# Matmuls in the source's order, finish and sample tokens as streams of their own, paired BK*AR

## The chip, the cores and the metric

The kernel runs on one core of one Trainium2 chip. The metric is device time in microseconds (us) of one execution. A core has TensorE (PE in the profile, its weight loads PEld), VectorE (DVE), ScalarE (ACT), GpSimd (POOL) and SyncE (SP, which here issues most DMAs). Each engine has an instruction stream of its own; semaphores order them. Matmuls write to PSUM, which has eight banks of 128 partitions x 512 float32.

## What is computed

One layer of a hybrid encoder on 1024 prompt tokens and 32 sample tokens. Cut to what matters:

```python
xn = rms_norm(x, norm_g)
proj = xn @ w_in                                   # 2048 -> 8320 columns
q, k, v, g_att, p_rw, g_rw = split(proj)
q, k = rope(rms_norm(q)), rope(rms_norm(k))        # 8 heads, two maps of 64 each
s = q @ k.T * 64 ** -0.5, masked by chunks of 64
p = softmax(s); attn = p[map 0] - lam * p[map 1]   # differential attention
o = rms_norm(attn @ v, subln_g) * (1 - lam_init)
att_out = o * silu(g_att)
# RWKV-7: per token, 16 heads of 64
S = S * w_t + (S @ a_t) b_t + v_t k_t;  y = S @ r_t
y = layer_norm(y) + bonus;  rw_out = y * silu(g_rw)
return x + [att_out, rw_out] @ w_out, and k, v, the last S, the last projected row
```

The sample tokens attend to 256 cached keys besides their own and begin from a given state.

## The kernel before

All data is float32 and lies with features on the partitions and tokens on the free axis. The tokens are done in two halves: the first (A) has prompt tokens 0 to 511 and the 32 sample tokens, 544 columns in two blocks of 288 and 256; the second (B) has prompt tokens 512 to 1023, 512 columns. `proj` multiplies a block of 128 output features by 16 blocks of the contraction. To keep the precision, weights and activations are split into a high and a low part in a faster matmul format (`wh`, `wl` in `split_w`, `xh`, `xl` in `split_x`), and each product is three matmuls: 96 matmuls a projection in A, 48 in B. Matmuls of plain float32 (those of the recurrence among them) appear as two records each, and transposes by PE as one.

The main loop goes over u = 0 to 15, eight heads of A and then eight of B. A head has eight projections in this order: q, k, v, attention's gate, the three inputs of the recurrence, its gate. After the heads come 16 output projections of A and 16 of B.

All other work of PE is woven into the projections. It is written as Python generators, queued in six streams: `chs` (`rw_chain`, the recurrence by chunks of 64 tokens), `dns` (`rw_down`, what a chain needs), `qks` (q, k and v), `pos` (`rw_post`), `ats` (`att_task`), `los` (`rw_decay`). A generator yields a delay, or a delay with a PSUM bank (`"am"` or `"Y"`), or a condition. The builder keeps a clock of PE's time, `clk`, to which each matmul adds its cost; a stream is taken up again when the clock has passed its delay and, if it named a bank, the time at which that bank is taken to be free. The delays stand in the table `LAT` in ns (line 39), by name and half: c1, c2, c3 are the three steps of a chain's cycle, for example. `pump` tries all streams; `proj` calls it every second or fourth block of the contraction and tries the chain's stream after each (lines 372 to 376). `drain` runs a stream until a named task is done, and moves the clock if it must; the loop drains attention of head u-1 after q's projection of head u (line 1006).

What the source does in this order is not the order in which PE works. The framework's scheduler orders the instructions of every engine when the program is built, by dependences and by its own estimate of times. So `LAT` gives the earliest place of a step and the scheduler may set it later.

The steps that the change touches:

- One cycle of `rw_chain` (lines 878 to 920): a matmul of `AR` with the state (`ch<-Sw,AR`); ACT copies `RS` from the bank (893), DVE adds `xs` in two instructions (896), ACT makes `SP` (899); a matmul `ch<-xs,TT` (901); ACT and DVE copy `UV` (902, 903); two matmuls `ch<-UV,MM` (906); DVE makes the new state `Sw` (908) and Y (916). Ahead of the cycles come transposes of v and three steps on 32 x 32 and 64 x 64 blocks (850 to 865), which wait for the solved blocks by DMA and a transpose on DVE (846).
- In `rw_down` `BK` times `AR` is done for four chunks at a time (754 to 768): first the four products of the partitions 0 to 63 into the bank Y, then, after Y is free, those of 64 to 127. DVE masks each result into MM (765). DVE then solves triangular systems in 31 steps of two instructions (784, 786).
- `att_task` goes over four query tiles of 128 in turn (527): scores into the two banks `sc`, softmax, the difference of the two maps (563), transposes into `sc` (570), a copy (571, 573), products with v into `am` (581), then `att_finish`. That squares the bank's values with a sum (504), takes the reciprocal root, multiplies by the row's factor (507), copies the bank with this scale (509), waits (511), transposes (513) and multiplies into `sg` (514). The next tile begins after it. In A the sample tokens follow as a fifth tile (583 to 618), in the buffer of E0.
- A PSUM tile is allocated anew for each use (`PT("am", 1)`, `PT("Y", 1)`, `PT("ch", 1)`, `PT("sc", 1)`), with one buffer a name.

```python
            elif isinstance(y, tuple):
                self.at, self.am = clk[0] + y[0], y[1]
```

Of the kernel before, what the change touches and what calls it, by code (L numbers as in the profile page):

```python
# [31 lines left out]
SCALE = 64 ** -0.5  # L32
# [6 lines left out]
LAT = dict(qkA=6246, qkB=2980, vA=9930, vB=9930, finA=1949, finB=3111, sc1A=1400, sc1B=1260, scAA=3566, scAB=3056, sc2A=3181, sc2B=3736, aTA=640, aTB=873, smp0A=2190, smp0B=3000, smp1A=4433, smp1B=7243, smp2A=1452, smp2B=1100, decA=3192, decB=6684, rnA=2646, rnB=1890, msA=8290, msB=8364, ms2A=2463, ms2B=1016, bk0A=1758, bk0B=1724, att0A=4044, att0B=1900, am2A=304, am2B=265, Y2A=1822, Y2B=1994, boA=1350, boB=3075, bktA=2250, bktB=2000, ttA=13941, ttB=14740, t10A=2258, t10B=1343, c0A=1052, c0B=2447, c1A=2162, c1B=1936, c2A=1122, c2B=978, c3A=1014, c3B=1276, postA=6000, postB=4636, dmA=5550, dmB=4110, solveA=31509, solveB=33325, am=900, Y=2208, scA=5863, sc1=2240, sc2=2872)  # L39
# [7 lines left out]
def build(tc, I, O):  # L47
# [18 lines left out]

    def am():
        ready["am"] = None
        return PT("am", 1)

    def ym():
        ready["Y"] = None
        return PT("Y", 1)
# [9 lines left out]
    def mm(out, lhsT, rhs, start=True, stop=True):  # L83
# [7 lines left out]
        clk[0] += max(0.4375 * n + 6.0, load) if rhs.dtype == F32R else 2 * max(0.84 * n, load)  # L91
# [12 lines left out]
    class Stream:  # L104
# [21 lines left out]
        def step(self):  # L126
# [20 lines left out]
            elif isinstance(y, tuple):  # L147
                self.at, self.am = clk[0] + y[0], y[1]
# [4 lines left out]
    chs, dns, los, qks, ats, pos = (Stream() for _ in range(6))  # L153
    streams = (chs, dns, qks, pos, ats, los)
# [346 lines left out]
    def att_finish(half, o_ps, m, il, sg, c0):  # L501
        oj = T([128, 128], "os", bufs=2)
        sm = T([128, 2], "sm", bufs=4)
        S.activation(oj[:m], o_ps, AF.Square, scale=il, accum_out=sm[:m, 0:1])
        rsqrt(sm[:m, 1:2], sm[:m, 0:1], 1.0 / 128, b_eps[:m])
        if not isinstance(il, float):
            V.tensor_tensor(sm[:m, 1:2], sm[:m, 1:2], il, op=ALU.mult)
        os_ = T([128, 128], "os", bufs=2)
        S.activation(os_[:m], o_ps, AF.Copy, scale=sm[:m, 1:2])
        ready["am"] = clk[0] + lat("fin", half)  # L510
        yield lat("fin", half), "am"
        pt = am()
        tr(pt[:, 0:m], os_[:m], ident[:m, :m])
        V.scalar_tensor_tensor(sg[:, c0:c0 + m], pt[:, 0:m], subg, sg[:, c0:c0 + m],
                               ALU.mult, ALU.mult)

    def att_task(half, h, st):
# [7 lines left out]

        yield lat("att0", half)
        for j in range(4):
# [7 lines left out]
            E = [T([128, 1024], "E0"), T([128, 1024], "E1")]  # L535
            mx = T([128, 2], "sm", bufs=4)
            l = T([128, 4], "l", bufs=2)
            if half == 0:
                sc = PT("sc", 1, (128, 2, 512))
# [9 lines left out]
            else:  # L549
                for c in range(2):  # L550
                    if c:
                        yield lat("sc1", half) + 2 * nk
                    sc = PT("sc", 1, (128, 2, 512)).rearrange("p a b -> p (a b)")
# [13 lines left out]
            aT = T([128, 8, 128], "E1")  # L567
            pt = PT("sc", 1, (128, 8, 128))
# [13 lines left out]
            yield from att_finish(half, po[:, :128], 128, l[:, 2:3], sg, qc)  # L582
        if half == 0:
            qb, ksm = st["qb"], st["ksm"]
            sm_ = T([128, 1024], "E0")
            ck = sm_[:, 0:256]
            dma(ck, I["ckT"][h])
# [572 lines left out]
```

## Time and profile before

| | |
|---|---|
| median of 3 runs | 2612.56 us (2609.12 to 2618.03) |
| the profiled execution, its own time | 2613.46 us |
| its span, first to last instruction | 2611.7 us |
| TensorE busy | 2549.7 us, 98% |
| weight loads busy | 2220.1 us, 85% |
| VectorE busy | 1892.0 us, 72% |
| ScalarE busy | 1349.6 us, 52% |
| GpSimd busy | 415.1 us, 16% |
| granted clock of TensorE, mean | 0.995 of full |

Matmuls are pipelined. The time of one in the profile includes its way through the array, with a modelled end, so the times of neighbours overlap, and a busy PE can still be late. The distance from one start to the next tells more than the duration. Idle time is given with what ended it, as far as the semaphores tell.

### The profile page before, as it was taken

The numbers are of one execution on the slowest core, as the hardware profiler recorded it, in microseconds if no ns is written. First come the engines' busy times: TensorE is split into PE (matmuls) and PEld (weight loads), VectorE is DVE, ScalarE is ACT, GpSimd is POOL, SyncE is SP. The second block draws the span as 40 slices with busy tenths as digits, with TensorE's granted clock in tenths as the row PEclk, the third lists the DMA queues.
The fourth block names the chain that finished last, engine by engine and source line by source line (L and its number), as shares of the span: only waits on it lengthen the run. The fifth ranks groups of instructions, "written<-read, shape, count | busy, mean of one in ns | idle before, by whom it ended". The sixth has DMA issues, their size and how long they took to land. (4 is left out here: it accounts for less than half of the span.)

```text
span 2611.7 us, 49090 instructions
## 1 busy us (share of the span) xinstructions
PE 2549.7 (98%) x17128; PEld 2220.1 (85%) x17128; DVE 1892.0 (72%) x5768; ACT 1349.6 (52%) x3138; POOL 415.1 (16%) x949
## 2 busy tenths in 40 slices
PE   7999999999999999999999999999999999999999
PEld 7999999999898999877777777777777778999887
DVE  7576877777777787788787887788878888753432
ACT  6455555555555655565555555555555556332321
POOL 3211111111111111111111111111111111111000
PEclk9999999999999999999999999999999999999999
DMA  4433332324242524353332323232324244544443
GB/s 156 119 102 94 93 103 84 110 82 115 75 122 80 170 72 122 98 153 100 98 98 87 103 83 106 85 111 81 114 81 115 77 132 118 176 148 140 137 142 108
DMA packets 198665, 286.74 MB, mean 110 GB/s; under 512 B 102097, under 2 KB 115921, under 8 KB 198417
## 3 DMA queue, kind: packets, MB, share of 16 engines
q0 software_dynamic: 51088, 169.12, 21.8%
q1 hardware_dynamic: 147328, 114.47, 15.5%
q8 instruction: 136, 2.23, 0.4%
q14 instruction: 113, 0.92, 0.1%
HBM read 228.11 MB, written 37.51 MB: 102 GB/s over the span
## 5 line engine op out<-in xcount | busy, mean ns | idle before, releaser
L92 PE MATMUL pj<-xh,wh 128*128 128x256 f32 (+2 forms) x3888 | 1294.2, 333 | 7.7 <-ACT xh L248 6.7
L92 PE MATMUL pj<-xl,wh 128*128 128x256 f32 (+2 forms) x3888 | 1274.7, 328 | 5.0 <-DVE xl L249 5.0
L92 PE MATMUL pj<-xh,wl 128*128 128x256 f32 (+2 forms) x3888 | 1272.5, 327 | 1.1 <-DVE wl L225 1.1
L92 PEld LDWEIGHTS pj<-xh,wh 128*128 128x128 f32 x3888 | 735.7, 189 | 61.2 <-ACT xh L248 7.0
L92 PEld LDWEIGHTS pj<-xl,wh 128*128 128x128 f32 x3888 | 736.2, 189 | 52.5 <-DVE xl L249 8.8
L92 PEld LDWEIGHTS pj<-xh,wl 128*128 128x128 f32 x3888 | 735.4, 189 | 52.4 <-DVE wl L225 2.1
L224 ACT CAST wh<-wr 128x512 fp32r<-128x512 f32 x584 | 360.6, 618 | 471.8 <-PE pj L92 420.1
L225 DVE TENSOR_TENSOR wl<-wr,wh 128x512 fp32r<-128x512 f32 x584 | 401.2, 688 | 193.5 <-ACT wh L224 162.9
L231 POOL DMA_DIRECT2D wr<-w_in x517 | 278.3, 538 | 1639.8 <-DVE wl L225 492.2
L786 DVE TENSOR_TENSOR ts<-tm,ts 64x54 f32<-64x54 f32 (+35 forms) x992 | 198.2, 200 | 15.1
L784 DVE TENSOR_TENSOR tm<-ts,ms 64x54 f32<-64x54 f32 (+35 forms) x992 | 197.7, 199 | 14.5 <-DMA ts<-tinit 0.2
L92 PEld LDWEIGHTS ch<-UV,MM 64*64 64x64 f32 (+2 forms) x1632 | 111.5, 145 | 38.1 <-DVE UV L903 9.2
L92 PE MATMUL ch<-UV,MM 64*64 64x64 f32 (+2 forms) x1632 | 128.9, 231 | 8.0 <-DVE UV L846 5.1
L899 ACT ACTIVATE SP<-Sw,PL 64x64 f32<-64x64 f32 x256 | 88.3, 345 | 91.2 <-DVE Sw L908 78.1
L225 DVE TENSOR_TENSOR wl<-MM,wh 128x512 fp32r<-128x512 f32 x64 | 44.0, 689 | 89.1 <-ACT wh L224 89.1
L224 ACT CAST wh<-MM 128x512 fp32r<-128x512 f32 x64 | 39.6, 620 | 128.9 <-PE pj L92 123.3
L896 DVE TENSOR_TENSOR xs<-ch,MM 64x64 f32<-64x64 f32 x272 | 58.6, 216 | 50.2 <-ACT RS L893 45.7
L908 DVE SCALAR_TENSOR_TENSOR Sw<-ch,PL,SP 64x64 f32<-64x64 f32 x256 | 70.7, 276 | 23.2 <-PE ch L92 16.7
L92 PE MATMUL am<-Vt,E 128*128 128x128 f32 (+1 forms) x592 | 84.7, 280 | 1.8 <-ACT wh L224 1.1
L92 PE MATMUL Y<-AR,BK 64*128 64x128 f32 x544 | 84.8, 290 | 0.7 <-DVE MM L765 0.6
L92 PEld LDWEIGHTS Y<-AR,BK 64*128 64x128 f32 x544 | 67.5, 188 | 19.8 <-issue 9.1
L92 PEld LDWEIGHTS am<-Vt,E 128*128 128x128 f32 (+1 forms) x592 | 73.5, 189 | 8.7 <-issue 2.6
(303 smaller groups left out, 3127.9 us busy)
## 6 DMA issues: line engine op xcount, KB each, us to landing
wr<-w_in POOLq DMA_DIRECT2D x517, 256.0 KB, 3.2
wr<-w_out POOLq DMA_DIRECT2D x64, 256.0 KB, 3.6
MM<-w_out POOLq DMA_DIRECT2D x32, 512.0 KB, 4.0
t<-xB SPq DMA_DIRECT2D x32, 256.0 KB
ms<-dm SPq DMA_DIRECT2D x96, 64.0 KB
t<-t SPq DMA_DIRECT2D x64, 68.0 KB
t<-mixd SPq DMA_DIRECT2D x16, 272.0 KB
t<-xA SPq DMA_DIRECT2D x16, 272.0 KB
```

What stands on the lines that cost most here:

```text
L92: PE.matmul(out, lhsT, rhs, start=start, stop=stop)
L224: S.copy(wh, raw)
L225: V.tensor_tensor(wl, raw, wh.bitcast(F32), op=ALU.subtract)
L231: q.dma_start(raw, wsrc[:, g * 512:(g + 1) * 512].rearrange("p (k f) -> p k f", k=4))
L784: V.tensor_tensor(tm, ts_[:, 0:qn, s:s + 1].to_broadcast([R * nb, qn, m]), ms[:, s:s + 1, s + 1:32].to_broadcast([R * nb, qn, m]), op=ALU. ...
L786: V.tensor_tensor(ts_[:, 0:qn, s + 1:32], tm, ts_[:, 0:qn, s + 1:32], op=ALU.add)
L896: V.tensor_tensor(xs[64 * h:64 * h + 64], ch[low, 64 * h:64 * h + 64], MM[low, c, h, 0:64], op=ALU.add)
L899: S.activation(SP[:, h, :], S_[hr, h, :], AF.Copy, scale=PL[hr, 0, gc:gc + 1])
L908: V.scalar_tensor_tensor(S_[hr, h, :], ch[low, 192 + 64 * h:256 + 64 * h], PL[low, h, gc:gc + 1], SP[:, h, :], ALU.mult, ALU.add)
```

## The change

PE's instructions are issued in the order of the source; the other engines are still ordered by the scheduler. The delays in `LAT` are set anew, most of them longer, a few shorter (t10A, t10B, c0B, Y2B), with new names for two steps (x0, bk). A wait may name two banks. Banks are allocated once and held. BK*AR alternates between the partitions 0 to 63, into Y, and 64 to 127, into `am`, and waits for both banks. The last part of `att_finish` becomes a task of a new stream, `fis`, and its first part reads the bank once and works on the copy. The sample tokens become a task of a new stream, `sms`, in parts of E0 and E1 that the first half's tiles do not use; `att_task` waits at its end for both. In the chain's cycle `xs` comes ahead of `RS`.

```diff
-LAT = dict(..., finA=1949, finB=3111, sc1A=1400, sc1B=1260, scAA=3566, ..., sc2B=3736, aTA=640, aTB=873, smp0A=2190, ..., smp1A=4433, ..., rnB=1890, ms2A=2463, ms2B=1016, bk0A=1758, bk0B=1724, ..., am2A=304, ..., ttA=13941, ttB=14740, t10A=2258, t10B=1343, c0A=1052, c0B=2447, c1A=2162, c1B=1936, c2A=1122, c2B=978, c3A=1014, c3B=1276, ..., am=900, Y=2208, ...)
+LAT = dict(..., finA=5000, finB=5000, sc1A=1400, sc1B=3600, scAA=8400, ..., sc2B=4400, aTA=2500, aTB=3000, smp0A=3600, ..., smp1A=9500, ..., rnB=6200, ms2A=2600, ms2B=3000, bk0A=7300, bk0B=6000, ..., am2A=2100, ..., ttA=27000, ttB=25500, t10A=1000, t10B=1000, c0A=1300, c0B=1700, c1A=2500, c1B=2300, c2A=2500, c2B=2500, c3A=1700, c3B=1800, ..., am=1500, Y=2208, ..., x0A=1000, x0B=1000, bkA=2600, bkB=3000)
...
+    held = {}
+    def bank(tag, shape=(128, 512)):
+        if tag not in held:
+            held[tag] = PT(tag, 1, shape)
+        return held[tag]
...
-            return max(self.at, ready[self.am]) if self.am else self.at
+            return max(self.at, *(ready[a] for a in self.am)) if self.am else self.at
...
-    chs, dns, los, qks, ats, pos = (Stream() for _ in range(6))
-    streams = (chs, dns, qks, pos, ats, los)
+    chs, dns, los, qks, ats, pos, fis, sms = (Stream() for _ in range(8))
+    streams = (chs, dns, qks, pos, fis, ats, sms, los)
...
-    def att_finish(half, o_ps, m, il, sg, c0):
+    def att_finish(half, h, name, o_ps, m, il, st, c0):
         oj = T([128, 128], "os", bufs=2)
+        S.activation(oj[:m], o_ps, AF.Copy, scale=il)
         sm = T([128, 2], "sm", bufs=4)
-        S.activation(oj[:m], o_ps, AF.Square, scale=il, accum_out=sm[:m, 0:1])
+        os_ = T([128, 128], "os", bufs=2)
+        S.activation(os_[:m], oj[:m], AF.Square, accum_out=sm[:m, 0:1])
         rsqrt(sm[:m, 1:2], sm[:m, 0:1], 1.0 / 128, b_eps[:m])
-        if not isinstance(il, float):
-            V.tensor_tensor(sm[:m, 1:2], sm[:m, 1:2], il, op=ALU.mult)
-        os_ = T([128, 128], "os", bufs=2)
-        S.activation(os_[:m], o_ps, AF.Copy, scale=sm[:m, 1:2])
-        ready["am"] = clk[0] + lat("fin", half)
-        yield lat("fin", half), "am"
-        pt = am()
-        tr(pt[:, 0:m], os_[:m], ident[:m, :m])
-        V.scalar_tensor_tensor(sg[:, c0:c0 + m], pt[:, 0:m], subg, sg[:, c0:c0 + m],
-                               ALU.mult, ALU.mult)
+        S.activation(os_[:m], oj[:m], AF.Copy, scale=sm[:m, 1:2])
+        def fin(born):
+            yield lambda: "sg" in st
+            yield max(0, born + lat("fin", half) - clk[0]), "am"
+            pt = am()
+            tr(pt[:, 0:m], os_[:m], ident[:m, :m])
+            sg = st["sg"]
+            V.scalar_tensor_tensor(sg[:, c0:c0 + m], pt[:, 0:m], subg, sg[:, c0:c0 + m],
+                                   ALU.mult, ALU.mult)
+        fis.add(("fin", half, h, name), fin(clk[0]))
...
+    def sample_task(h, st):
+        Et, qb, ksm, Vt = (st[a] for a in ("Et", "qb", "ksm", "Vt"))
+        ck = Et[0][:, 512:768]
...
+        att_finish(0, h, 4, po[0:32, :128], 32, 1.0, st, 256)
...
+        if half == 0:
+            sms.add(("smp", h), sample_task(h, st))
...
             yield lat("aT", half), "am"
-            if j == 0:
-                yield lambda: "sg" in st
-                sg = st["sg"]
-                yield lat("am2", half), "am"
...
-            yield from att_finish(half, po[:, :128], 128, l[:, 2:3], sg, qc)
+            att_finish(half, h, j, po[:, :128], 128, l[:, 2:3], st, qc)
...
-        dma(mixd[half][h], sg)
+            yield lambda: ("smp", h) in sms.done
+        yield lambda: all(("fin", half, h, j) in fis.done for j in range(5 - half))
+        dma(mixd[half][h], st["sg"])
...
+            yield lat(key, half), "Y", "am"
+            key = "ms2"
+            ps2 = (ym(), am())
+            for j in range(m):
+                for h, hr in enumerate((low, high)):
+                    mm(ps2[h][:, 128 * j:128 * j + 128],
+                       BK[hr, c0 + j].rearrange("p a t -> p (a t)"),
+                       AR[hr, c0 + j].rearrange("p a t -> p (a t)"), ways=2)
             for h in range(2):
-                yield lat(key, half), "Y"
-                key = "ms2"
-                hr = (low, high)[h]
-                p = ym()
-                for j in range(m):
-                    mm(p[:, 128 * j:128 * j + 128],
...
             mm(ch[:, 0:128], AR[:, c].rearrange("p a t -> p (a t)"), Sf)
-            RS = T([128, 128], "RS")
-            S.copy(RS[high], ch[high, 0:128])
             xs = T([128, 64], "xs")
             for h in range(2):
                 V.tensor_tensor(xs[64 * h:64 * h + 64], ch[low, 64 * h:64 * h + 64], MM[low, c, h, 0:64], op=ALU.add)
+            RS = T([128, 128], "RS")
+            S.copy(RS[high], ch[high, 0:128])
...
     with tile.TileContext(nc) as tc:
-        build(tc, I, O)
+        with tc.manual_schedule(engines={mybir.EngineType.PE}):
+            build(tc, I, O)
```

## Rows read from the trace of the kernel before

**Rows 1.** The page: the span, and busy time of each engine.

```profile
span 2611.7 us, 49090 instructions
...
PE 2549.7 (98%) x17128; PEld 2220.1 (85%) x17128; DVE 1892.0 (72%) x5768; ACT 1349.6 (52%) x3138; POOL 415.1 (16%) x949
```

**Rows 2.** Table of stretches: stretch, length, busy us of each engine, clock, DMA.

```profile
260.00:700.00 440.00, 430.00 (x3465) 402.91 (x3464) 333.36 (x1096) 237.42 (x596) 73.15 (x187) 1.00 0.33 95
1300.00:1800.00 500.00, 489.52 (x2715) 385.26 (x2713) 400.94 (x1261) 274.73 (x633) 74.82 (x164) 0.99 0.33 95
2450.00:2600.00 150.00, 150.00 (x651) 121.97 (x651) 45.73 (x68) 34.00 (x55) 13.72 (x26) 1.00 0.43 135
```

**Rows 3.** The chain that ended last, its last two links: start, length, what.

```profile
2342.09 265.94 PE pj L92 x1476
2608.05 0.69 DVE t L968
```

**Rows 4.** Timeline of PE around one BK*AR: start us, length us, what.

```profile
1571.45 0.39 PE L92 MATMUL pj<-xl,wh 128*128 128x512 f32 x1
1571.67 0.40 PE L92 MATMUL pj<-xh,wl 128*128 128x512 f32 x1
1572.00 1.16 PE L92 MATMUL Y<-AR,BK 64*128 64x128 f32 x8
1573.09 0.50 PE L92 MATMUL pj<-xh,wh 128*128 128x512 f32 x1
1573.43 0.40 PE L92 MATMUL pj<-xl,wh 128*128 128x512 f32 x1
```

**Rows 5.** List of waits: who waited for whom, us in total, times, longest.

```profile
DVE xs L896 <- ACT RS L893: 45.7, 40, 4.2
...
PE ch L92 <- DVE xs L896: 7.0, 16, 1.6
PE pj L92 <- ACT xh L248: 6.7, 1, 6.7
...
PE ch L92 <- DVE UV L846: 5.1, 7, 1.2
```

**Rows 6.** Groups by line and shape, PE: BK*AR.

```profile
L92 PE MATMUL Y<-AR,BK 64*128 64x128 f32 x544 | 84.8, 290 | 0.7 <-DVE MM L765 0.6
```

**Rows 7.** Timeline of PE, second half, without the projections: chain and attention.

```profile
1746.67 0.68 PE L92 MATMUL ch<-UV,MM 64*64 64x64 f32 x16
...
1748.24 0.46 PE L92 MATMUL ch<-Sw,AR 128*128 128x128 f32 x2
1750.40 0.41 PE L92 MATMUL ch<-xs,TT 128*128 128x64 f32 x2
...
1753.72 0.57 PE L92 MATMUL ch<-UV,MM 128*128 128x64 f32 x4
...
1756.13 1.06 PE L92 MATMUL am<-Vt,E 128*128 128x128 f32 x8
...
1760.56 0.48 PE L92 MATMUL sc<-Ks,Qd 128*128 128x512 f32 x1
...
1761.22 0.27 PE L97 MATMUL am<-cst,os 128*128 128x128 f32 x1
```

**Rows 8.** Timeline of DVE after the BK*AR of rows 4.

```profile
1578.25 0.68 DVE L765 TENSOR_TENSOR MM<-Y,cst 128x512 f32<-128x512 f32 x1
```

**Rows 9.** Timeline of ACT and of DVE in the cycle of rows 7.

```profile
1748.74 0.26 ACT L893 COPY RS<-ch 64x128 f32<-64x128 f32 x1 [0.60 <-PE ch L92]
...
1750.08 0.22 DVE L896 TENSOR_TENSOR xs<-ch,MM 64x64 f32<-64x64 f32 x1
...
1753.29 0.23 DVE L903 COPY UV<-ch 64x64 f32<-64x64 f32 x1
...
1754.84 0.28 DVE L908 SCALAR_TENSOR_TENSOR Sw<-ch,PL,SP 64x64 f32<-64x64 f32 x1
```

**Rows 10.** Timeline of PE at the end of head 11's attention.

```profile
1697.28 0.33 PE L97 MATMUL am<-cst,os 128*128 128x128 f32 x1
...
1699.07 0.39 PE L92 MATMUL pj<-xh,wh 128*128 128x512 f32 x1
```

More of the change, by code (lines that the diff above doesn't have):

```diff
@@ L65, in build, with scores2 @@
     ready = {"am": 0.0, "Y": 0.0}
+    held = {}
[3 more added lines that the diff above has]
+        return held[tag]
     def am():
         ready["am"] = None
-        return PT("am", 1)
+        return bank("am")
     def ym():
         ready["Y"] = None
-        return PT("Y", 1)
+        return bank("Y")
+    def scores2():
+        return bank("sc", (128, 2, 512))
     mode = [(128, 128)]
@@ L81, in shaped, with mm @@
             mode[0] = now
-    def mm(out, lhsT, rhs, start=True, stop=True):
+    def mm(out, lhsT, rhs, start=True, stop=True, ways=1):
         n, m = 1, 1
@@ new lines, in sample_task @@
+    def sample_task(h, st):
+        Et, qb, ksm, Vt = (st[a] for a in ("Et", "qb", "ksm", "Vt"))
+        ck = Et[0][:, 512:768]
+        dma(ck, I["ckT"][h])
+        cv = Et[0][:, 768:1024].rearrange("p (j d) -> p j d", j=2)
+        dma(cv, I["cv"][:, h, :].rearrange("(j p) d -> p j d", p=128))
+        yield lat("smp0", 0), "am"
+        p = am()
+        mm(p[0:64, 0:256], qb, ck)
+        mm(p[0:64, 256:288], qb, ksm)
+        sx = T([64, 4], "sx")
+        V.tensor_reduce(sx[:, 0:1], p[0:64, 0:288], AX.X, ALU.max)
+        V.tensor_scalar(sx[:, 0:1], sx[:, 0:1], -SCALE, None, ALU.mult)
+        es = Et[1][0:64, 512:800]
+        S.activation(es, p[0:64, 0:288], AF.Exp, bias=sx[:, 0:1], scale=SCALE,
+                     accum_out=sx[:, 1:2])
+        V.reciprocal(sx[:, 2:3], sx[:, 1:2])
+        cmb = T([64, 32], "cmb")
+        V.tensor_scalar(cmb, idst, sx[:, 2:3], lamcol, ALU.mult, ALU.mult)
+        yield lat("smp1", 0), "am"
+        p = am()
+        for j in range(3):
+            m = 128 if j < 2 else 32
+            mm(p[:m, 32 * j:32 * j + 32], es[:, 128 * j:128 * j + m], cmb)
+        at = Et[1][:, 800:896].rearrange("p (j q) -> p j q", j=3)
+        V.tensor_copy(at[:, 0:2, :], p[:, 0:64].rearrange("p (a b) -> p a b", a=2))
+        V.tensor_copy(at[0:32, 2, :], p[0:32, 64:96])
+        yield lat("smp2", 0), "am"
+        po = am()
+        for j in range(3):
+            if j < 2:
+                mm(po[0:32, :128], at[:, j, :], cv[:, j, :], start=(j == 0), stop=False)
+            else:
+                mm(po[0:32, :128], at[0:32, 2, :], Vt[0:32, 4, :], start=False)
+        att_finish(0, h, 4, po[0:32, :128], 32, 1.0, st, 256)
@@ L794, in rw_down @@
             m = min(4, cn - c0)
-            yield lat("ms2", half), "Y"
+            yield lat("bk", half), "Y"
             p = ym()
@@ L822, in rw_chain @@
         yield lat("bk0", half)
-        p = PT("ch", 1)
+        p = bank("ch")
         for j in range(2):
@@ L847, in rw_chain @@
         yield max(1500, t_m + lat("tt", half) - clk[0])
-        p = PT("ch", 1)
+        p = bank("ch")
         for g in range(ng):
@@ L852, in rw_chain @@
         yield lat("t10", half)
-        p = PT("ch", 1)
+        p = bank("ch")
         for g in range(ng):
@@ L858, in rw_chain @@
             S.copy(TT[64 * h:64 * h + 32, :, 64 * h + 32:64 * h + 64], pg[:, :, h, :])
-        yield lat("t10", half)
-        p = PT("ch", 1)
+        yield lat("x0", half)
+        p = bank("ch")
         for c in range(cn):
```

58 lines of the change are left out of this document (11 added, 47 removed).

## The prediction

> **What bounds the kernel now.** The page comes first: TensorE (PE) is busy 2549.7 of 2611.7 us, VectorE (DVE) 1892 and ScalarE (ACT) 1350 [rows 1]. PE's ends are modelled, so the next view is the table of stretches: PE has almost no idle time in a stretch of the first half of the tokens and in one of the second, and none at the end [rows 2]. Whether a busy PE is also at its rate shows in the chain that ended last: its last link is 1476 projection matmuls in 265.94 us, 708 of them of the first half (288 and 256 columns) and 768 of 512 columns [rows 3]. In the timeline the starts of 512-column matmuls lie 0.23 us apart (from 1571.45 to 1571.67) [rows 4], which leaves 0.125 us for each of the 708. That is the undisturbed rate. All 7776 + 3888 projection matmuls at it cost 972 + 897 = 1869 us. The other 5464 matmul records (17128 in all [rows 1]) have spacings that the timeline shows in the same way, such as 0.112 us for a 128-column pass of a float32 matmul; counted over all shapes they give about 505 us. Ahead of the first matmul lie 6.7 us and behind the last some 4 [rows 3, 5], so some 2601 - 2374 = 227 us are neither.
>
> Where those 227 us are: the PE stream leaves the projections 991 times for a small step. One such excursion can be read in [rows 4]: 0.33 us from the last projection matmul to the first of Y, where 0.23 is its own, and on return 0.34 in place of 0.23. So going there and back costs about 0.2 us there, less elsewhere, and 991 of them make some 150 us that no order takes away. The rest is waiting. Comparing every start with the one before, over all 17128 records and with 0.095 us let pass for the change of shape, I find 288 places that are late by more than 0.015 us and 71 us in all: 41 before matmuls that write the chain's bank `ch`, 10 before `am`, 7 before `sc`, 3 before Y and 10 before projections (7 of these in the first 33 us). The page's own idle time, 62 us, is the same thing seen coarser. The list of waits has the names, `xs` and `UV` from DVE ahead [rows 5]. So the change can win at most the 71 us of waiting and what it takes off PE's work; all else is hidden behind PE.
>
> **The paired BK*AR.** The 544 records are 272 float32 matmuls of two passes, contracting over 64 partitions [rows 6]. Eight of these records run from 1572.00 to about 1572.90, so 0.112 us each [rows 4]. The change alternates rows 0-63 and rows 64-127 and gives each its own bank. No pair of this kind is in the trace. The nearest is line 863, two matmuls that share rows 64-127 and write to different partitions: 16 records took 0.68 us with the modelled end of the last one (0.22), so 0.029 us each [rows 7], where a single pass of 64 columns would need about 0.058. They overlap fully. I take a factor of two for the new pair: a full group of 16 records falls from 1.79 to 0.95 us, 32 such groups give 27 us, the 8 small ones 1. Bounds: 0 (the halves don't overlap) to -30; I take -27. Since two visits become one, 40 of the 991 excursions go: 40 x 0.15 = -6 us.
>
> What the pair costs is a bank. `am` serves q/k norms, v, the products with v, finishes, sample and posts, and until now BK*AR never touched it. Its second half is emptied by DVE (line 765) in 0.68 us, and DVE's queue is in order: of the group in [rows 4] the last matmul ended by 1573.1 and line 765 began at 1578.25 [rows 8]. The new plan lets the next user of `am` come 1.5 us after. That is the slower rival, below. The row says that emptying is late by queueing, not by rate, since groups come 40 times in 2200 us. The Trainium skill (TensorEngine Tiling (Array Packing), Performance Considerations, PSUM Bottleneck) says that tiling speeds up TensorE but not the emptying of PSUM, which may then be the limit. By that a group would cost two emptyings, 1.36 us, in place of 0.95, and the saving would be some 15 us, not 27: the sum below would then be 2570.
>
> **PE in the source's order, with new delays.** Before, the framework's scheduler placed PE's instructions by its own estimates; the delays in LAT were only the earliest moments. Now the order is that of the source, so a delay that is too short stops PE and everything queued behind: the projections, and so all other streams. What the chain needs can be read in one cycle. `ch<-Sw,AR` starts at 1748.24; RS is copied from 1748.74 to 1749.00; the second `xs` ends at 1750.30; `ch<-xs,TT` starts at 1750.40, 2.16 us on. The second UV copy waits in DVE's queue until 1753.29, and `ch<-UV,MM` starts at 1753.72, 3.3 us on. The second Sw ends at 1755.12, 1.4 us on [rows 7, 9]. Over the 136 cycles the time from a step's start to its data is 1.5 us in the median and 2.7 at the ninth decile for c2, 1.0 and 2.3 for c3, 1.1 and 2.4 for c1. The new delays are 2.5, 1.7 (1.8 in the second half) and 2.5 (2.3): they cover some 80 to 90 in 100 cycles, where the old ones of 1.1, 1.0 and 2.2 covered few. If DVE's queue stayed as it is, the late cycles would add 17 + 10 + 9 = 36 us (a stream is looked at only every three matmuls, 0.28 us later on the mean, which is taken off). Two things shorten it: `xs` comes ahead of RS, and ACT's RS was what DVE waited for in 40 cases, 45.7 us [rows 5]; and the wait for the solved blocks is 12 us longer, which covers the steps that waited for line 846 (5.1 us of idle PE [rows 5]). I take 41 -> 27 on `ch`. Below: 41 -> 10; above: 41 -> 60.
>
> Longer delays lengthen the streams. A chain cycle becomes 6.7 us, a chain some 40, and a head has two. A head takes at most 140 us (the span less 32 output blocks at the rate, 370 us, over 16 heads): no drain is reached. In attention the scores of the next tile (1760.56) start some 3.5 us after the product with v that began at 1756.13, together with the finish's transpose (1761.22) [rows 7]. With the finish as a stream of its own the scores follow the product at once; that gives 3.5 us back, and the longer sc1, sc2 and aT delays take about as much. Sample tokens beside the tiles shorten the first half's attention. Both lie behind PE: zero, as long as `att` ends before the next head's q is through. There is little room: the last finish of head u=11 starts at 1697.28 and the next head's k at 1699.07 [rows 10]; if it were missed by 4 us in each of 8 heads, 32 us.
>
> **The rest.** The finish reads its bank once (Copy) and not twice with Ln, Exp and a multiply between, so `am` is free earlier; ACT gets 72 more copies, at most 0.7 us each (DVE's 512 columns [rows 8]; these have 128), 50 us on an engine with 1262 us idle [rows 1]: zero. For `am`, `sc`, Y and projections I take 30 -> 22 us of waiting. Banks held once change no order by themselves: the next writer still waits for the last reader; zero, bounds -5 to +10.
>
> **Sum** on the profiled execution (2613.5 us; its span 2611.7; the median of the runs shown is 2612.6): -27 - 6 - 14 - 8 = -55, so 2558 us.
>
> **The rivals.**
> Waiting stays at 71 us: the delays trade one tail for another. Then 2613.5 - 33 = 2580. For it: the ninth deciles above, which the queue of DVE sets, 72% busy with solve steps in between. Against: the wait for RS goes.
> Waiting nearly vanishes, 71 -> 20: 2613.5 - 33 - 51 = 2530. For it: the deliberate room in aT, fin and tt. Against: 7 us of it is the start, and the tails reach 6 us.
> Slower: the bank `am` after a pair. Each of 40 pairs stops PE until DVE has emptied both halves, if an `am` step is due. From a group's last matmul to the end of line 765 it was 1.3 us in the median of the first half's groups, 2.0 in the second's, and 5.9 in [rows 4, 8]; two emptyings follow one another now, 0.7 more. At 2 us for each pair the 80 us outweigh the 55; with the other steps as forecast that gives 2640. It decides from 1.4 us a pair. Against: not each pair has an `am` step behind it at that moment, and DVE goes on while PE stands.
> The change doesn't pair: rows as before (0) but waiting down 22: 2585; it lies in the first rival's bounds.
>
> **How the numbers follow.** Chances: forecast (2540 to 2570) 0.43; waiting unchanged or no pairing (2570 to 2604) 0.21; waiting nearly gone (below 2540) 0.12; within 0.3%, about what a measurement can tell (2604.7 to 2620.4), as a mixture of gain and `am` loss, 0.08; slower by the bank 0.16. So faster 0.76, same 0.08, slower 0.16. The range goes from 2508 (all waits gone) to 2635, and leaves out the worse half of the slower rival.
>
> **What would show it.** Right: Y<-AR,BK and its partner on `am` 0.056 us apart; idle PE down from 62 towards 45 us; `xs` no longer behind RS; no wait on line 846. Wrong: PE idle before `am` named by line 765; waits on `xs`, UV, Sw longer than 41 us in sum; projections that wait at the start of k of the next head.

## The result and the profile after

The changed kernel takes 2792.7 us (median of four runs, 2789.3 to 2796.3) where the kernel before took 2612.6: ratio 1.069, interval 1.066 to 1.071. Slower by 180 us; the forecast was 2558 and the range ended at 2635.

The page of the kernel after, which answers to [rows 1]: span, busy times, then PE by slices of 70 us and the clock granted to it.

```profile
span 2787.5 us, 48869 instructions
...
PE 2547.7 (91%) x17128; PEld 2270.1 (81%) x17128; DVE 1912.1 (69%) x5704; ACT 1380.2 (50%) x3210; POOL 412.1 (15%) x949
...
PE   4999989999899899888988898999999999999999
...
PEclk9999999999989899998999999999999999999999
```

By the page PE is busy as long as before (2547.7 against 2549.7 us) in a longer span, so the page shows the new time as idle. The first slice shows a 4, and ten of those between 350 and 1750 us an 8. The table of stretches answers to [rows 2], and the last long link of the chain that ended last to [rows 3].

```profile
260.00:700.00 440.00, 407.91 (x3416) 391.27 (x3414) 330.06 (x1049) 237.03 (x606) 72.59 (x186) 0.98 0.33 93
1300.00:1800.00 500.00, 450.02 (x2419) 367.50 (x2418) 364.13 (x1128) 256.37 (x590) 65.75 (x146) 0.93 0.30 84
2600.00:2750.00 150.00, 150.00 (x675) 122.78 (x674) 53.99 (x83) 40.21 (x68) 14.85 (x28) 1.00 0.45 142
```

```profile
2571.93 211.92 PE pj L102 x1044
```

In the second half's heads PE is busy 450 of 500 us, not 489.5, and its mean clock is 0.93, not 0.99. The output blocks at the end run as before. So the loss lies in the heads, in two forms: PE stands, and what it does between stops is slower. PE's list of waits says behind whom it stands, where [rows 5] had at most 7.0 us, behind `xs`:

```profile
PE ch L102 <- ACT RS L911: 57.2, 32, 4.5
PE am L102 <- DVE p L317: 32.9, 1, 32.9
PE ch L102 <- DVE Yt L931: 18.6, 11, 3.3
PE am L107 <- DVE Yt L952: 17.7, 6, 5.2
PE am L102 <- DVE MM L780: 16.5, 11, 5.1
...
PE am L107 <- DVE MM L780: 5.8, 5, 1.9
```

Made up by the prediction's own method (every start against the one before, over all 17128 records; a stop is what a matmul with a wait is late beyond 0.095 us), the 176 us by which the span grew divide thus: the first matmul starts 26 us later (32.9 against 6.7 us), the stops are 221 us against 71, in the stretches at half the clock (granted 0.5, that is 1.2 GHz) PE's other starts lie 94 us behind the plain rate of their shapes, against 8, and the rest is 86 us less: 26 + 150 + 86 - 86 = 176. The last term holds the pair's 24 us and fewer trips to and from the projections (808, not 991, because several steps now follow one another). At the prediction's 0.15 us a trip those are 27 us, so some 35 us of this term stay unaccounted for.

**Where PE has nothing to do but steps.** Before, 5 gaps between two projection matmuls were over 3 us, 20 us in all, the longest 6.1. After, 45 are, 340 us in all, the longest 21.5. PE's timeline in that one, which is the second half's second head, between the recurrence's first and second input:

```profile
1429.47 0.39 PE L102 MATMUL pj<-xh,wl 128*128 128x512 f32 x1
1429.79 0.69 PE L102 MATMUL ch<-k,UV 32*32 32x32 f32 x16
1430.41 0.77 PE L107 MATMUL sc<-cst,E 128*128 128x128 f32 x5
...
1433.87 0.39 PE L102 MATMUL ch<-Sw,AR 128*128 128x128 f32 x2
1438.51 0.43 PE L102 MATMUL ch<-xs,TT 128*128 128x64 f32 x2 [4.25 <-ACT RS L911]
...
1449.24 1.49 PE L107 MATMUL sc<-cst,E 128*128 128x128 f32 x6
1450.38 0.56 PE L102 MATMUL Y<-p,blkr 128*128 128x256 f32 x1
1450.74 0.41 PE L102 MATMUL Y<-kk,blkr 128*128 128x256 f32 x1
1450.95 0.63 PE L102 MATMUL pj<-xh,wh 128*128 128x512 f32 x1
```

This is a `drain`. The source asks here, after the first of the three inputs (line 1046), for the end of `rw_down` of the head before; it is not due, so the builder puts down whatever step is, and where none is due it moves its clock ahead. Added up over the build, `clk` is moved by 115 us so: 88 at this drain (11.1 us for the head shown), 19 where the recurrence's v waits for the chain of the head before (1050), 8 elsewhere. In the kernel before it was 1.9 us. These are called planned jumps below.

### The profile page after: what moved, and what is told of

The parts are those of the page before. It is cut to its first block, busy times and chain, and to the rows that moved or that the text cites. A ratio compares the mean times of both kernels' runs of the same rounds, so it can differ in the third digit from the quotient of the medians.

```text
span 2787.5 us, 48869 instructions
## 1 busy us (share of the span) xinstructions
PE 2547.7 (91%) x17128; PEld 2270.1 (81%) x17128; DVE 1912.1 (69%) x5704; ACT 1380.2 (50%) x3210; POOL 412.1 (15%) x949
## 4 chain that ended last, share of the span: by engine, by line
PE 48%; DVE 11%; issue 4%; ACT 4%; DMA 4%; SPq 0%; POOL 0%; DVEq 0%; ACTq 0%; POOLq 0%
PE pj L102 37%; PE ch L102 4%; PE am L102 2%; PE sc L102 2%; DVE wl L235 2%; DVE ts L801 1%; DMA wr<-w_out 1%; DVE tm L799 1%; PE Y L102 1%; PE sc L107 1%; DMA wr<-w_in 1%; ACT wh L234 1%; PE am L107 1%; DVE MM L780 0%; DVE sm L608 0%
## 5 line engine op out<-in xcount | busy, mean ns | idle before, releaser
L102 PE MATMUL pj<-xh,wh 128*128 128x256 f32 (+2 forms) x3888 | 1336.3, 344 | 10.6 <-DVE t L361 5.6
L102 PEld LDWEIGHTS pj<-xh,wh 128*128 128x128 f32 x3888 | 750.2, 193 | 65.0 <-DVE t L361 6.8
L102 PEld LDWEIGHTS pj<-xh,wl 128*128 128x128 f32 x3888 | 749.2, 193 | 61.0 <-DVE wl L235 1.5
L102 PEld LDWEIGHTS pj<-xl,wh 128*128 128x128 f32 x3888 | 751.1, 193 | 43.9
L102 PEld LDWEIGHTS ch<-UV,MM 64*64 64x64 f32 (+2 forms) x1632 | 122.1, 152 | 51.6 <-issue 18.0
L102 PEld LDWEIGHTS ch<-xs,TT 128*128 128x128 f32 x272 | 46.4, 199 | 75.1 <-ACT RS L911 71.3
L102 PE MATMUL ch<-xs,TT 128*128 128x64 f32 x272 | 52.5, 276 | 57.6 <-ACT RS L911 57.2
L102 PEld LDWEIGHTS am<-Vt,E 128*128 128x128 f32 (+1 forms) x592 | 79.8, 207 | 23.1 <-DVE MM L780 8.9
```

The costliest lines, as they stand in the source:

```text
L102: PE.matmul(out, lhsT, rhs, start=start, stop=stop)
```

## The experiments

All waits are ns of `LAT`. Line numbers are those of the kernel after. "Stops" and "half clock" are counted as above. The time is the median of the runs; the other columns are of the profiled execution, and planned jumps are those of the build.

| kernel | time us | planned jumps | first matmul at | stops | at half clock (stretches) | its cost |
|---|---|---|---|---|---|---|
| before | 2612.6 | 1.9 | 6.7 | 71 | 26 (4) | 8 |
| after | 2792.7 | 115 | 32.9 | 221 | 268 (48) | 94 |
| e1, scheduler | 2573.4 | 115 | 6.9 | 88 | 37 (7) | 12 |
| e2, RS first | 2768.3 | 115 | 33.6 | 212 | 198 (36) | 69 |
| e3, before with the pair | 2601.2 | 7.3 | 7.1 | 99 | 80 (11) | 27 |
| e4, before in source order | 2870.4 | 1.9 | 34.0 | 256 | 271 (46) | 94 |
| e5, c1 to c3 longer | 2927.4 | 464 | 33.4 | 318 | 450 (53) | 129 |
| e7, priorities | 2744.6 | 115 | 34.1 | 192 | 240 (34) | 79 |
| e9, tt and attention short | 2719.7 | 2.8 | 33.4 | 194 | 134 (28) | 47 |
| e10, chain short | 2797.8 | 11.6 | 33.3 | 224 | 183 (32) | 81 |
| e14, attention short | 2851.4 | 124 | 33.6 | 266 | 322 (47) | 106 |
| e15, all in one | 2745.8 | 2.8 | 7.0 | 222 | 224 (42) | 80 |
| e16, scheduler, old waits | 2572.2 | 4.9 | 6.7 | 74 | 15 (4) | 5 |
| e17, before, new waits | 2701.8 | 447 | 7.2 | 154 | 172 (10) | 30 |
| e18, less work on DVE | 2734.7 | 115 | 33.8 | 182 | 234 (41) | 82 |

**e1: PE left to the scheduler, all else as changed.**

```diff
-        with tc.manual_schedule(engines={mybir.EngineType.PE}):
-            build(tc, I, O)
+        build(tc, I, O)
```

> The changed kernel with PE ordered by the framework's scheduler again; streams, delays, banks, pairs and the swap of xs and RS stay. Theory A (the source's order stops PE wherever a delay is too short): the 180 us go, 2570 to 2610 us, idle PE below 65 us, granted clock 0.99. Theory B (RS copied after xs is the cause, since ch<-xs,TT waits for both): about 60 us of waiting stay, 2640 to 2680. Theory C (the new delays and streams are the cause): 2750 or more.

Measured 2573.4 us (2571.5 to 2576.4), ratio to the kernel before 0.985 (0.983 to 0.987). That is theory A: the order of the source costs 219 us, and everything else in the change gains 39. From e1 to the changed kernel the span grows by 216 us: 26 of start, 133 of stops, 82 of half clock, less 25 for fewer trips. The row of the page for PE by slices, where every slice but the first now has a 9:

```profile
PE   7999999999999999999999999999999999999999
```

**e4: the kernel before with the source's order alone; e3: with the pair alone.**

```diff
+        with tc.manual_schedule(engines={mybir.EngineType.PE}):
```

> The kernel before with PE in the source's order and nothing else; its delays are the short old ones. Theory A: the chain's steps come 1 to 3 us too early in most of the 136 cycles and each stops PE; more than the changed kernel's loss: 2900 us or more, granted clock below 0.95. Theory C: the order costs little, below 2650.

> The kernel before with the paired BK*AR alone (into Y and am, waiting for both). If the pair runs side by side and the bank am costs nothing: -27 us for the records and some -6 for 40 visits, 2575 to 2590 us. If am after a pair is the bound (the slower rival of the prediction): 2620 to 2640.

e4 took 2870.4 us (two runs; 1.099, 1.094 to 1.104), a little under theory A's 2900: the order costs the old waits 258 us, though they plan next to no jumps (1.9 us). Short waits turn into stops, here behind `xs`:

```profile
PE ch L92 <- DVE xs L896: 62.7, 28, 4.4
```

e3 took 2601.2 us (0.996, 0.994 to 0.998), 11 us less, which misses the 2575 to 2590 expected. On PE the pair did save what it should: the records of BK*AR took 45.9 us from start to start where they had taken 79.9. In e3's profile stops rose from 71 to 99 us and the time at half the clock from 26 to 80 us, which takes most of that back.

**e2: RS ahead of xs again. e7: priority on DVE and ACT for xs, RS, UV, Sw and Yt. e6: the norms by blocks (`rb_a`, `rb_b`) behind the first projection of each half.**

```diff
+            RS = T([128, 128], "RS")
+            S.copy(RS[high], ch[high, 0:128])
             xs = T([128, 64], "xs")
...
-            RS = T([128, 128], "RS")
-            S.copy(RS[high], ch[high, 0:128])
```

```diff
+            with tc.high_priority():
                 xs = T([128, 64], "xs")
...
```

```diff
-    rb_a()
-    ready["am"] = clk[0]
...
+        (rb_a, rb_b)[half]()
+        ready["am"] = clk[0]
```

> The changed kernel with RS copied ahead of xs, as before. Theory A: PE still stops at its other early steps; the 57 us of idle PE named by RS shrink, but waits on xs come in their place: 2740 to 2790. Theory B: RS ceases to be what ch<-xs,TT waits for and the clock stays up: 2690 or less.

> The changed kernel with a higher scheduling priority for the chain's instructions on DVE and ACT (xs, RS, both UV copies, both Sw, Y): they go ahead of q's rotation and the solve steps that now stand before them in these queues. Theory A3 (the waits on ch are the place of those instructions in the in-order queues): waiting on ch falls from 119 us to 60 or less, 2710 to 2740 us. Rival A1 alone (the delays are shorter than the bare latency): 2780 or more.

> The changed kernel with the norm's column sums (rb_a, rb_b) issued behind the first projection of each half and not ahead of it. In the changed kernel PE's first matmul of a projection starts at 36.3 us, before at 6.7, and that projection ends 15 us later. Theory A (the source puts a matmul that waits for all of x ahead of work that could run): 15 us less at the start and some 8 at the second half, 2765 to 2775 us. If the start is hidden later (by the loads of weights or by the streams): 2788 to 2796.

e2 took 2768.3 us (1.059, 1.057 to 1.062), 24 less than the changed kernel; e7 2744.6 (1.051, 1.048 to 1.053), 48 less, just over the 2710 to 2740 expected; e6 2788.9 (1.067, 1.065 to 1.070), 4 less. The last is a miss: the first matmul starts at 7.0 us again, 26 earlier, and the time is given back, to 10 us more of stops and 13 more at the half clock. What an earlier start wins is mostly lost later.

In e2 and e7 the stops move more than they go. In e2 those on `ch` are 114 us where the changed kernel has 119, now behind `xs` first, as theory A had it; what falls is the time at half the clock. In e7 those on `ch` fall to 35 us, further than the 60 expected, but those on `am` rise from 63 to 105.

**e5: c1, c2 and c3 longer by 2 us.**

```diff
-LAT = dict(..., c1A=2500, c1B=2300, c2A=2500, c2B=2500, c3A=1700, c3B=1800, ...)
+LAT = dict(..., c1A=4500, c1B=4300, c2A=4500, c2B=4500, c3A=3700, c3B=3800, ...)
```

> The changed kernel with the six delays of the chain's cycle (c1, c2, c3 of both halves) 2 us longer. Theory A1 (a delay that is too short stops PE): the 119 us of waiting before matmuls on ch fall to 50 or less, the clock rises, 2700 to 2730 us. Rival A2 (the streams get too long, the loop's drains come into the way, or the tails of DVE's queue move along): 2780 or more.

2927.4 us (1.120, 1.117 to 1.123), 135 more. The chain's waits are not too short in a way that longer ones would mend: they make the streams late and the drains longer (464 us planned).

**e9, e10, e13, e14: shorter waits, with fewer planned jumps in three of them.** In this order: e13, e14 (e9 is both), e10.

```diff
-LAT = dict(..., ttA=27000, ttB=25500, ...)
+LAT = dict(..., ttA=13941, ttB=14740, ...)
...
-LAT = dict(..., finA=5000, finB=5000, sc1B=3600, scAA=8400, aTA=2500, aTB=3000, smp0A=3600, smp1A=9500, am=1500, ...)
+LAT = dict(..., finA=1949, finB=3111, sc1B=1260, scAA=3566, aTA=640, aTB=873, smp0A=2190, smp1A=4433, am=900, ...)
...
-LAT = dict(..., sc1B=3600, scAA=8400, c0A=1300, c0B=1700, c1A=2500, c1B=2300, c2A=2500, c2B=2500, c3A=1700, c3B=1800, ...)
+LAT = dict(..., sc1B=1260, scAA=3566, c0A=1052, c0B=2447, c1A=2162, c1B=1936, c2A=1122, c2B=978, c3A=1014, c3B=1276, ...)
```

> The changed kernel with nothing altered but waits: tt as in the kernel before (13941 and 14740 for 27000 and 25500), and attention's and the sample's waits aT, scA, sc1B, smp0A, smp1A, fin and am as before; the chain's c0 to c3, t10, x0, bk0 stay. On the program's own clock the time that it jumps over in a drain, because nothing is due, falls from 115 us to 2.8 us. Theory D (the longer waits leave the planner with nothing to place, and in the source's order PE stands there): each planned us cost 0.4 us when 2 us were put on c1 to c3 (348 us more planned, 135 us more measured), so 112 us fewer give some -45 us, about 2750 us, and if the jumps cost their full length 2680 us. Theory S (PE in a fixed order stops for whatever DVE and ACT do later than planned; a short wait turns a planned jump into a stop): the stops on ch and am grow by what the jumps lose, and the time is 2780 to 2860 us.

> The changed kernel with nothing altered but waits: the chain's c0 to c3 and attention's scA and sc1B as in the kernel before, tt and all others as changed. The clock's jumps fall from 115 us to 11.6 us, and none is left at the solve's end of the unit before (the drain for down). Theory D: -40 to -100 us, 2690 to 2750 us. Theory S: the chain's stops (PE on ch behind RS, xs, Yt: 119 us of stops on ch in the changed kernel) grow instead, 2780 to 2860 us. If D holds here and not with tt short, tt's length was worth having.

> The changed kernel with tt alone as before (13941 and 14740). Planned jumps 115 to 71 us, those for the solve's end of the unit before gone, attention's 68 us new. Theory D (planned jumps cost about 0.65 us each, as 73 us for 112): -29 us, 2764 us. Rival (tt's length was a mistake of its own, and attention's waits do nothing): 2720 us, as with both. Rival (attention's waits carry it): 2790 us.

> The changed kernel with attention's and the sample's waits alone as before (aT, scA, sc1B, smp0A, smp1A, fin, am), tt as changed. Planned jumps 124 us, where the changed kernel has 115. Theory D: no gain, 2785 to 2800 us. If attention's waits carry the 73 us: 2720 to 2740 us.

e9 took 2719.7 us (1.041, 1.038 to 1.043), 73 less than the changed kernel: 27 us less of stops and 47 of half clock. But e10, with 11.6 us planned, took 2797.8 (1.069, 1.067 to 1.072), no less; e13 2784.2 (1.064, 1.059 to 1.068); e14 2851.4 (1.089, 1.085 to 1.093), 59 more. Waits of e10 and e14:

```profile
PE ch L102 <- ACT RS L911: 76.9, 61, 5.6
```

```profile
PE am L107 <- DVE Yt L952: 33.6, 11, 8.3
PE ch L102 <- ACT RS L911: 28.2, 22, 2.9
PE ch L102 <- DVE UV L918: 25.0, 17, 6.0
```

Neither theory carries all four. With short chain waits the jumps go and the stops behind RS take their place (57 to 77 us); that is the rival's case. With tt and attention's waits short together the gain is real, and neither half has it alone. So a planned jump has no fixed price.

**e15: all that saved time, in source order** (e9, e7, e2 and e6 together).

> The changed kernel, PE still in the source's order, with all that took time off one by one: tt and attention's waits as before (-73), priority for xs, RS, UV, Sw and Yt on DVE and ACT (-48), RS ahead of xs (-24, partly the same time as the priority's), the norms of k by blocks behind the first projection of each half (-4). If these add up: 2645 to 2670 us, still 70 to 100 us over the scheduled form, and this rest belongs to the fixed order itself. Rival (planned jumps and queue tails are the whole cost of the fixed order): 2580 to 2600 us.

2745.8 us (1.049, 1.044 to 1.054): 26 more than e9 alone. The savings don't add. Stops are 222 us as in the changed kernel, in other places: 42 on `ch` where it had 119, but 68 on `sc` (8 before) and 37 on Y (19). The fastest kernel in source order is e9, at 2720.

**e18: the same order, plan and waits, less work on DVE.** DVE is busy in 191 of the 221 us of stops: some 28 us of that are the low part of the weights (235), 37 the solve (799, 801), 20 the rotation's last lines (450, 456). In e18 the low part of the weights is computed for the first three blocks only, and their three low parts serve for all later ones, so the output leaves out that correction.

```diff
-        wl = T([128, 4, 128], "wl", F32R, bufs=3)
...
-        V.tensor_tensor(wl, raw, wh.bitcast(F32), op=ALU.subtract)
-        return wh, wl
+        i = nw[0] % 3
+        nw[0] += 1
+        if nw[0] <= 3:
+            WL[i] = T([128, 4, 128], f"wl{i}", F32R)
+            V.tensor_tensor(WL[i], raw, wh.bitcast(F32), op=ALU.subtract)
+        return wh, WL[i]
```

> The changed kernel in source order, and the low part of the weights left out: the first three blocks are computed, and every later block's matmuls use one of these three. DVE loses 642 or so instructions of 0.69 us, some 445 of 1912 us; PE's instructions, their order and the waits in LAT are the same, and ACT still writes the high part. Theory Q (PE's stops are the length of DVE's in-order queue, seen through an order that can't give way): the stops, 221 us, fall by more than the 28 us in which the subtraction itself runs inside them, to 120 us or less, the granted clock rises from 0.952 to 0.97 or more, and the time is 2640 to 2690 us. Theory F (the fixed places and the planned jumps set the stops, however busy DVE is): the 28 us go, 2750 to 2770 us.

DVE's busy time fell from 1912 to 1531 us (381 us, not the 445 expected), and the time to 2734.7 us (1.047, 1.045 to 1.049), 58 less: between the two theories, nearer to F. The stops fell by 39 us, some 11 more than ran inside them. DVE's queue is a part of the cost; 182 us of stops stay with a fifth of its work gone.

**The same tail under both orders.** What the order does is seen where q's rotation (lines 447 to 456) stands in DVE's queue ahead of a chain's `xs`. In the kernel after (PE, then DVE, then ACT):

```profile
2260.51 0.38 PE L102 MATMUL ch<-Sw,AR 128*128 128x128 f32 x2
...
2263.26 0.39 PE L102 MATMUL pj<-xh,wl 128*128 128x512 f32 x1
2268.12 0.43 PE L102 MATMUL ch<-xs,TT 128*128 128x64 f32 x2 [4.47 <-ACT RS L911]
```

```profile
2261.80 0.69 DVE L447 TENSOR_TENSOR t<-t,cos 128x512 f32<-128x512 f32 x1
...
2266.21 0.69 DVE L456 TENSOR_TENSOR Ql<-t,Qd 64x512 fp32r<-64x512 f32 x1
...
2267.56 0.22 DVE L909 TENSOR_TENSOR xs<-ch,MM 64x64 f32<-64x64 f32 x1
```

```profile
2267.81 0.26 ACT L911 COPY RS<-ch 64x128 f32<-64x128 f32 x1 [1.85 <-DVE xs L909]
```

And in e1, in the same place of an earlier head, PE and ACT:

```profile
1795.70 0.38 PE L102 MATMUL ch<-Sw,AR 128*128 128x128 f32 x2
...
1802.83 0.40 PE L102 MATMUL pj<-xh,wh 128*128 128x512 f32 x1
1805.95 0.43 PE L102 MATMUL ch<-xs,TT 128*128 128x64 f32 x2 [2.73 <-ACT RS L911]
```

```profile
1805.64 0.26 ACT L911 COPY RS<-ch 64x128 f32<-64x128 f32 x1 [1.51 <-DVE xs L909]
```

RS is later in e1 (9.9 us after the matmul, 7.3 in source order), yet PE loses less: the scheduler, which orders all engines by its estimates, put 31 projection matmuls between the two steps, the source's order 12. Over all 136 cycles RS begins 1.94 us after the matmul's second pass in the median and 3.49 at the ninth decile in source order, 1.8 and 4.05 in e1: the data come no sooner. The late cycles show the difference. In source order the data of `ch<-xs,TT` (both `xs` and RS) are written more than 4 us after the first matmul in 14 cycles; these have 12 projection matmuls in between in the mean, no more than the others (14), and stop PE for 2.8 us each, 39 us in all. In e1 it is 19 cycles; these have 23 in between where the others have 13, and the stops are 0.7 us each, 13 us in all. PE is elsewhere meanwhile. A wait in `LAT` is one number for all cycles.

**e8, e11, e12, e16, e17: what gains the 39 us.** e8 is e1 with RS first (the edit of e2), e11 e1 with the priorities of e7, e12 e1 with the pair's two members in two loops, e16 e1 with all waits as before, e17 the kernel before with the new waits alone.

```diff
-            for j in range(m):
-                for h, hr in enumerate((low, high)):
+            for h, hr in enumerate((low, high)):
+                for j in range(m):
```

> The changed kernel with PE ordered by the scheduler (2573 us) and RS ahead of xs as before. If the swap loses in either order (RS behind xs and ACT's queue, 16.5 us of idle PE with the scheduler's order): 2555 to 2565 us. If the scheduler's order hides it: 2570 to 2577.

> The changed kernel with PE left to the scheduler (2573 us so far) and with xs, RS, the UV copies, Sw and Yt given priority on DVE and ACT, as took 48 us from the changed kernel in source order. Theory A (in source order each queue tail on DVE stops PE, and the scheduler fills such a stop with projections): here the priority finds little to save, 2560 to 2573 us; stops on ch, 44 us, fall by some 10. Rival (the chain's queue tails cost the same in either order): -40 us, 2530 us.

> The changed kernel with PE left to the scheduler and the pairing undone: the two members of BK*AR in two loops, h outside, in the same two banks. If the pairing carries the gain of the scheduled form over the kernel before (39 us), the time is 2600 us or more; the pair alone gave the kernel before 11 us, so if the rest is in the streams and the waits, 2580 to 2590 us.

> The changed kernel with PE left to the scheduler and all waits of LAT as in the kernel before (x0 as t10, bk as ms2 there). If the new waits bring the 39 us, about 2610 us; if the streams of the finish and of the sample tokens and the bank read once bring them, about 2573 us.

> The kernel before, PE left to the scheduler, with the new waits of LAT alone. If the waits bring the scheduled form's 39 us, about 2573 us; if the streams do, 2613 us or more, since longer waits with the finish inside attention's stream make attention longer.

e8 2570.3 us (0.983, 0.981 to 0.986), e11 2573.8 (0.985, 0.982 to 0.987), e12 2572.7 (0.985, 0.982 to 0.987), e16 2572.2 (0.985, 0.982 to 0.988): all as e1. So under the scheduler neither the swap, nor the priorities, nor the waits make a difference, one by one.

e12 does not show the same of the pair, because the two loops did not undo it: the scheduler laid the members side by side again in part, as PE's timeline of e12 shows:

```profile
146.34 0.27 PE L102 MATMUL am<-AR,BK 64*128 64x128 f32 x1
146.34 0.27 PE L102 MATMUL Y<-AR,BK 64*128 64x128 f32 x1
146.45 0.27 PE L102 MATMUL am<-AR,BK 64*128 64x128 f32 x1
146.45 0.27 PE L102 MATMUL Y<-AR,BK 64*128 64x128 f32 x1
```

Of the 272 pairs that are possible, 97 start within 0.04 us of each other in e12, 231 in e1 and none in the kernel before; the 544 records take 60, 49 and 80 us from start to start.

What divides the gain is e3 against e16, both with the scheduler and the old waits: the pair alone takes 11 us off the kernel before, and the pair with all the rest 40. So 29 us belong to the finish and the sample tokens as streams of their own, the finish's single read of its bank and the banks held once, together with the swap, which e8 finds without effect. In both the records of BK*AR take 46 us, but e16's stops are 74 us and its time at half the clock 15, where e3 has 99 and 80: what the pair saves on PE is not given back there. The parts were not taken apart, and the streams without the pair were not run.

e17 took 2701.8 us (1.034, 1.030 to 1.038): the new waits with the finish still inside attention's stream plan 443 us of jumps for attention's end (line 1006 of the kernel before), and PE, in the scheduler's order too, has steps without projections between them:

```profile
PE ch L92 <- DVE Yt L916: 44.0, 24, 4.6
```

The kernels around 2572 us are faster than the kernel before by 1.5 to 1.7%.

## Why the prediction was wrong, point by point

**The bound** held for gains only. It put what can be won at the waiting and what comes off PE's work. e16 fits that: its stops are 74 us, hardly other than before, and its span is 44 us shorter, of which the records of BK*AR are 34 (46 us for 80) and the trips some 9 (929 for 991, at 0.15 us). The bound says nothing of what can be lost, and the prediction priced losses only at `ch`, at `am` behind a pair and at attention's end.

**The pair** was right in the trace. PE's timeline, to set beside [rows 4, 6]:

```profile
1736.88 0.27 PE L102 MATMUL Y<-AR,BK 64*128 64x128 f32 x1
1736.88 0.27 PE L102 MATMUL am<-AR,BK 64*128 64x128 f32 x1
1736.99 0.27 PE L102 MATMUL Y<-AR,BK 64*128 64x128 f32 x1
1736.99 0.27 PE L102 MATMUL am<-AR,BK 64*128 64x128 f32 x1
```

Partners start within 0.01 us of each other and pairs 0.11 us apart, 0.056 a record as forecast. The 544 records took 55.5 us start to start where they took 79.9: 24 us for the 27 forecast. As time the pair gave 11 us alone (e3). The step that failed is that what PE saves is saved as time: e3 saved 34 us on PE and gave most of it back in stops and at half the clock. The rule drawn on there, the Trainium skill (TensorEngine Tiling (Array Packing), Performance Considerations, PSUM Bottleneck), would have left 15 us by the prediction's estimate. The trace bears out its direction, not its size: on PE 24 us went, and the emptying (line 780) is named for 16.5 + 5.8 us of idle PE on `am`.

**"41 -> 27 on `ch`"** is the first step that failed: the stops on `ch` are 119 us. It took the delays to cover 80 to 90 cycles in 100 and priced the others one by one at their lateness, 36 us less what the swap and tt save. The swap saved nothing: in every one of the 136 cycles RS now begins behind the second `xs` (ACT's list of waits has 82.5 us for that, where [rows 5] have 45.7 us the other way round), and `ch<-xs,TT` writes to the bank that both read, so it waits for both. From the second pass of `ch<-Sw,AR` to `ch<-xs,TT` it is 2.87 us in the median, of which the delay is 2.5, where it was 1.73. Undoing the swap gives 24 us back (e2), though the stops on `ch` stay. And a late cycle stops PE, not just the chain: 14 cycles make 39 of the 61 us of stops before `ch<-xs,TT`.

**"30 -> 22 us" for `am`, `sc`, Y and projections** failed in the same way: 63 + 8 + 19 + 12 = 102 us. That sentence had no row behind it of how an order that can't give way treats those steps; e4 shows it with the old waits (87 us on `am`).

**"No drain is reached"** failed. It compared a chain of 40 us with a head of 140 and forgot what comes ahead of the chain: `rw_down`, whose own end waits in the queue and is asked for early in the next head. 115 us of planned jumps, 88 of them at this drain, show that it is reached. The gaps alone would not: e4 has 47 of them, 231 us in all, with 1.9 us of planned jumps. Nor are the drains the whole cost: e4 is slower, and e10, with 11.6 us planned, is no faster.

**Attention behind PE at zero** held in the changed kernel, where no jump is planned for attention, but only because tt made the recurrence later still: with tt short, 68 us are planned for it (e13), and with the old streams 443 (e17). The little room that [rows 10] show was the right thing to look at.

**What it left out.** `rb_a` stands ahead of the first projection in the source, so PE's first matmul starts at 32.9 us where the projection of the kernel before started at 6.7. This cost 4 us in the end (e6).

```profile
32.89 1.27 PE L102 MATMUL am<-asg,p 128*128 128x272 f32 x2 [32.89 <-DVE p L317]
```

And the clock: matmuls at its lower level cost 86 us more than before, a term the sum did not have.

**The rivals.** The one that ended slower had the bank `am` behind a pair at 80 us; line 780 is named for 22. It had the right sign by a wrong mechanism: the kernel before, which has no pair, becomes 258 us slower in the source's order (e4). The rival that was missing is a sentence of the prediction itself, that a short delay "stops PE and everything queued behind", carried to all of PE's steps, not to the chain's alone.

**What stayed right or untested.** ACT's copies and the banks held once at zero: ACT grew by 31 us of busy time, and PE's list of waits has the finish's copies (`os`, line 518) for 0.8 us. The banks were not tried alone. Of the signs of being right, three came true: 0.056 us a record for the pair, `xs` no longer behind RS, and no wait on the transpose of line 846 (861 after). The fourth did not: PE's idle time on the page went from 62 to 240 us. What stays open is how the 219 us of the source's order divide further: short waits (73 us), priorities (48) and less DVE work (58) each take time off the changed kernel, and the first two with e2's and e6's edits together only 47.

## What to carry to other kernels

To hand an in-order engine's order to the source is to promise when every other engine will be done, at every step: price all its waits, not those of one bank, and ask how late the queue of the busiest other engine can be at the worst place (here 7 to 10 us behind a rotation), because one number for a wait is either too short there or too long elsewhere. Before costing longer waits at nothing, add up each stream from the first step to the point where the source asks for its end. And test a bundle with its order alone undone first: one run showed here that the order cost 219 us and the rest had gained 39. Where a scheduler may put back what a run takes out, look in its trace whether it is out (e12).

## What the runs showed of the hardware

In the kernel after the clock fell behind a stop. Around the one at 2263 us (stretch, length, busy times, clock, DMA), and PE's matmuls behind it:

```profile
2250.00:2263.00 13.00, 13.00 (x64) 10.82 (x64) 9.63 (x31) 7.89 (x17) 2.15 (x4) 1.00 0.34 109
2263.00:2268.00 5.00, 0.65 (x3) 0.19 (x1) 4.84 (x15) 1.80 (x4) 0.54 (x1) 1.00 0.44 117
2268.00:2274.00 6.00, 5.88 (x22) 4.88 (x23) 4.27 (x18) 2.06 (x6) 0.34 (x1) 0.72 0.13 35
```

```profile
2269.70 0.63 PE L102 MATMUL pj<-xl,wh 128*128 128x512 f32 x1
2270.13 0.63 PE L102 MATMUL pj<-xh,wl 128*128 128x512 f32 x1
...
2272.79 0.40 PE L102 MATMUL pj<-xl,wh 128*128 128x512 f32 x1
2273.02 0.39 PE L102 MATMUL pj<-xh,wl 128*128 128x512 f32 x1
```

PE does nearly nothing for 5 us, and it is when it works again that the granted clock is 0.72, a mean of 1.2 and 2.4 GHz: 512-column matmuls start 0.43 us apart (2269.70, 2270.13), 0.23 from 2272.79 on. The time at the lower level does not follow the sum of the stops: e9 has 194 us of stops and 134 us at the lower level, the changed kernel 221 and 268. In the gap of 21.5 us shown above the mean clock was 0.73.

The members of a pair on the upper and lower 64 rows start together although each is a float32 matmul of two passes: the pair costs what one cost before, 0.11 us a pass.
